# One written order for the step from the mixer's output to the feed-forward part

## The chip, the core and the metric

The kernel runs on one core of a Trainium2 chip. TensorE multiplies matrices, VectorE and ScalarE work on tiles, GpSimd does some element work and issues some of the loads, SyncE issues the others. Five engines run side by side, each through its own queue in order. The metric is the device time of one execution in microseconds; lower is better.

## The reference, cut to what matters

One layer over 256 tokens of width 2048, in float32. `attn` and `ssm` are the two halves of the mixer, `rms_norm` divides by the root of the mean square over the width and multiplies by a weight per feature.

```python
mixed = jnp.concatenate([attn, ssm], axis=-1) @ w_out[l]
x = x + rms_norm(mixed, ln_mix_post[l])
h = rms_norm(x, ln_ffn_pre[l])
u = causal_depthwise_conv(h @ w_ffn_up[l], ffn_conv_w[l], ffn_conv_b[l])
gate, up = jnp.split(u, [FFN_HIDDEN], axis=-1)
f = (jax.nn.gelu(gate, approximate=True) * up) @ w_ffn_down[l]
x = x + rms_norm(f, ln_ffn_post[l])
```

The change lies between the first line and the fourth: a product with `w_out`, a norm, a sum, a second norm, a product with `w_ffn_up`.

## The kernel before

Tokens are two tiles of 128 (`t` = 0, 1). Every product in float32 is made of three: weights and features are each split into a high and a low part of a shorter format, and high x high, high x low and low x high are summed in PSUM. Weights come in units of 128 x 1024 (0.5 MB), in the order in which they are used. `Weights.split` (L60) does one unit: SyncE loads it into a raw buffer (ring of four, `raw`), ScalarE rounds it to the high part (`whi`, L63), VectorE subtracts to get the low part (`wlo`, L64); `whi` and `wlo` are rings of four too. `tick()` follows each unit that TensorE has used: it fetches the next one, and issues work that was put off by a count of units (`defer`).

Two forms of product occur. `rows_part` (L253) multiplies a unit with token tile `t`, six matmuls of 512 columns, the output being tokens x 512 features; a chunk of 512 output features takes eight units of `w_out`. `cols_part` (L180) gives 128 output features x 256 tokens: for each of 16 slices of the width a matmul of 512 columns (high and low features of both token tiles) and one of 256. `cols_tok` (L187) does the same by token tile: one matmul of 256 columns for tile 0, two for tile 1. An up tile (`cols_tile`) takes two units.

The output `mixed` is made in four chunks. While they run, `post` (L738) squares and sums each (ScalarE) and multiplies it by the norm's weight into `mm` (VectorE). GpSimd multiplies `mm` by the second norm's row `lnrow` for three chunks of token tile 1 (`weighted`, L772). In the last chunk `rows_staggered` (L275) holds eight units: first all of token tile 0, then token tile 1. To hold eight, the chunk's first four units go to buffers of their own (`own`, L732). `last_post` (L744) is what follows for one token tile: the last sum of squares, the factor 1/rms (`late_rsqrt`: VectorE, a power on GpSimd, VectorE), `x1 = mm * r + x` in four pieces, and times `lnrow`: for token tile 0 on GpSimd (L761), for token tile 1 from the parts made ahead on GpSimd (L752, L768). `features` (L779) transposes a piece in four on TensorE (L782), ScalarE copies the high part out and VectorE the low part (L171, L172). The factor of the second norm is the same for a whole token and so is applied after the up product: `second_rms` (L785) finds it, `along_tokens` (L156) spreads it along the tokens (`rb2`) with two transposes on TensorE. `cols_pair` (L235) begins the first two up tiles with token tile 0; `gated` (L866) does convolution and gelu of a pair.

What sets the order: the code is written as one sequence, and a planner puts each engine's instructions into its queue, by the written order among those that it reckons to be ready; it may therefore run later work first. `tc.issue_after(i)` keeps instructions behind `i` on its engine. At the kernel's end the last chunk of the feed-forward output uses `rows_staggered` too, and `fdone` writes each token tile out.

## Time and profile before

| what | value |
|---|---|
| time, median of 3 runs | 1140.27 us (1140.26 to 1141.01) |
| the profiled execution | 1140.66 us |
| its span, first to last instruction | 1138.90 us |
| TensorE busy in the span | 99% |
| VectorE busy | 792.9 us, 70% |
| ScalarE busy | 592.9 us, 52% |
| GpSimd busy | 30.8 us, 3% |
| mean granted TensorE clock | 0.997 of full speed |

The span is that of one profiled execution; 1.76 us of that execution lie outside it. Busy shares are means over stages: what a stage waits for is read from the waits and the sequence in it. The last output chunk runs from about 359 to 383 us of the span, the first up tiles from 387 us on. TensorE's weight loads run beside its matmuls and have rows of their own (PEld). Matmuls overlap in the pipeline, so the time from one start to the next is the price of one, not the duration shown.

### The profile page before, as it was taken

The numbers are of one execution on the slowest core, as the hardware profiler recorded it, in microseconds if no ns is written. First come the engines' busy times: TensorE is split into PE (matmuls) and PEld (weight loads), VectorE is DVE, ScalarE is ACT, GpSimd is POOL, SyncE is SP. The second block draws the span as 40 slices with busy tenths as digits, with TensorE's granted clock in tenths as the row PEclk, the third lists the DMA queues.
The fourth block names the chain that finished last, engine by engine and source line by source line (L and its number), as shares of the span: only waits on it lengthen the run. The fifth ranks groups of instructions, "written<-read, shape, count | busy, mean of one in ns | idle before, by whom it ended". The sixth has DMA issues, their size and how long they took to land.

```text
span 1138.9 us, 15739 instructions
## 1 busy us (share of the span) xinstructions
PE 1127.2 (99%) x5896; PEld 957.2 (84%) x5896; DVE 792.9 (70%) x1250; ACT 592.9 (52%) x913; POOL 30.8 (3%) x32
## 2 busy tenths in 40 slices
PE   9999999999999899999999999999999999999997
PEld 7877888888888788888888888888888888888886
DVE  6587886776655988777878644447878787865562
ACT  6555544554454575555555444335555555554451
POOL 0000000000010500000000000000000000000000
PEclk9999999999999999999999999999999999999999
DMA  8756444555597275566656556656556656656662
GB/s 306 281 167 199 140 155 137 184 168 167 171 329 238 75 245 186 185 187 187 190 190 189 185 186 188 189 194 186 185 187 186 191 188 191 186 185 186 189 216 74
DMA packets 60148, 215.53 MB, mean 189 GB/s; under 512 B 7119, under 2 KB 7800, under 8 KB 59176
## 3 DMA queue, kind: packets, MB, share of 16 engines
q1 hardware_dynamic: 58696, 207.69, 57.2%
q0 software_dynamic: 1088, 6.48, 1.6%
q8 instruction: 46, 0.75, 0.3%
q10 hardware_dynamic: 288, 0.35, 0.1%
q14 instruction: 30, 0.25, 0.1%
HBM read 212.39 MB, written 2.11 MB: 188 GB/s over the span
## 4 chain that ended last, share of the span: by engine, by line
PE 94%; DVE 2%; DMA 2%; issue 1%; ACT 1%; SPq 0%; POOL 0%; POOLq 0%; ACTq 0%; DVEq 0%
PE pa L183 36%; PE pa L184 18%; PE pa L258 8%; PE pa L260 8%; PE pa L259 8%; PE ph L259 4%; PE ph L260 4%; PE ph L258 4%; DVE wlo L64 1%; DMA raw<-in_wout_dram 1%; PE pab L183 1%; PE pa L191 1%; DMA raw<-in_win_dram 1%; PE py L567 1%; PE pab L184 1%
## 5 line engine op out<-in xcount | busy, mean ns | idle before, releaser
L64 DVE TENSOR_TENSOR wlo<-raw,whi 128x1024 fp32r<-128x1024 f32 (+1 forms) x377 | 465.2, 1235 | 261.1 <-ACT whi L63 260.4
L63 ACT CAST whi<-raw 128x1024 fp32r<-128x1024 f32 (+1 forms) x377 | 395.1, 1048 | 455.6 <-PE pa L183 174.6
L183 PE MATMUL pa<-h,whi 128*128 128x512 f32 x1376 | 483.3, 394 | 0.0
L184 PE MATMUL pa<-h,wlo 128*128 128x256 f32 x1376 | 389.2, 283 | 0.0
L183 PEld LDWEIGHTS pa<-h,whi 128*128 128x128 f32 x1376 | 258.4, 188 | 59.6
L184 PEld LDWEIGHTS pa<-h,wlo 128*128 128x128 f32 x1376 | 258.7, 188 | 0.0
L183 PE MATMUL pa<-hT,whi 128*128 128x512 f32 x384 | 138.5, 399 | 0.0
L184 PE MATMUL pa<-hT,wlo 128*128 128x256 f32 x384 | 108.2, 283 | 0.0
L823 DVE SCALAR_TENSOR_TENSOR cfc<-cfu,fcv,cfc 128x255 f32<-128x255 f32 (+1 forms) x176 | 84.7, 481 | 4.5 <-ACT cfc L821 1.5
L183 PEld LDWEIGHTS pa<-hT,whi 128*128 128x128 f32 x384 | 72.2, 188 | 16.6 <-issue 0.2
L184 PEld LDWEIGHTS pa<-hT,wlo 128*128 128x128 f32 x384 | 72.1, 188 | 0.3 <-issue 0.2
L260 PE MATMUL pa<-whi,gT 128*128 128x512 f32 x176 | 69.5, 395 | 0.0
L258 PE MATMUL pa<-whi,gT 128*128 128x512 f32 x176 | 69.4, 395 | 0.0
L259 PE MATMUL pa<-wlo,gT 128*128 128x512 f32 x176 | 69.4, 394 | 0.0
L259 PE MATMUL ph<-wlo,gT 128*128 128x512 f32 x160 | 63.1, 395 | 0.0
L260 PE MATMUL ph<-whi,gT 128*128 128x512 f32 x160 | 63.1, 395 | 0.0
L258 PE MATMUL ph<-whi,gT 128*128 128x512 f32 x160 | 63.1, 395 | 0.0
L821 ACT ACTIVATE cfc<-cfu,fcv 128x256 f32<-128x256 f32 x88 | 52.6, 597 | 1.4 <-DVE cfu L820 1.4
L258 PE MATMUL pa<-whi,hT 128*128 128x512 f32 x128 | 51.7, 404 | 0.2 <-DVE xsT L200 0.2
L260 PE MATMUL pa<-whi,hT 128*128 128x512 f32 x128 | 50.7, 396 | 0.0
L259 PE MATMUL pa<-wlo,hT 128*128 128x512 f32 x128 | 50.6, 395 | 0.0
L258 PE MATMUL pa<-whi,mT 128*128 128x512 f32 x112 | 43.9, 392 | 0.0
(242 smaller groups left out, 1183.6 us busy)
## 6 DMA issues: line engine op xcount, KB each, us to landing
raw<-in_wup_dram SPq DMA_DIRECT2D x176, 512.0 KB, 3.5
raw<-in_wdown_dram SPq DMA_DIRECT2D x88, 512.0 KB, 3.5
raw<-in_win_dram SPq DMA_DIRECT2D x87, 512.0 KB, 3.5
raw<-in_wout_dram SPq DMA_DIRECT2D x32, 512.0 KB, 4.3
xsq<-in_x_dram SPq DMA_DIRECT2D x2, 1024.0 KB, 7.8
xt<-in_x_dram POOLq DMA_DIRECT2D x2, 1024.0 KB, 7.5
xr<-in_xT_dram SPq DMA_DIRECT2D x7, 256.0 KB, 6.2
out_dram<-xt SPq DMA_DIRECT2D x6, 256.0 KB, 2.4
```

The source lines that it names most:

```text
L63: nc.scalar.copy(hi[:, s], raw[:, s])
L64: nc.vector.tensor_tensor(lo[:, s], raw[:, s], f32(hi[:, s]), op=ALU.subtract)
L183: nc.tensor.matmul(ps, w[0][:, s], aT[:, k, :, :], start=(k == 0), stop=False)
L184: end[0] = nc.tensor.matmul(ps[:, :S], w[1][:, s], aT[:, k, 0, :], start=False, stop=(k == KT - 1)).ins
L191: nc.tensor.matmul(both, w[0][:, s], aT[:, k, :, tok(t)], start=(t == 0 and k == 0), stop=False)
L258: nc.tensor.matmul(ps, a, w[0][:, s], start=(first and j == 0), stop=False)
L259: nc.tensor.matmul(ps, a, w[1][:, s], start=False, stop=False)
L260: end[0] = nc.tensor.matmul(ps, b, w[0][:, s], start=False, stop=(last and j == 1)).ins
L567: nc.tensor.matmul(py[:, i * 64:(i + 1) * 64], rows[:, t, g, i, :], xcs[t, g][:, i * 64:(i + 1) * 64], start=True, stop=True)
L821: nc.scalar.activation(c, u, AF.Identity, scale=wv[:, 2:3], bias=wv[:, 3:4])
L823: nc.vector.scalar_tensor_tensor(c[:, sh:], u[:, :S - sh], wv[:, 2 - sh:3 - sh], c[:, sh:], op0=ALU.mult, op1=ALU.add)
```

## The change

The step from the last output chunk to the third up tile is written out as one sequence for TensorE, ScalarE and VectorE inside `tc.manual_schedule`, which fixes their order. All products with `lnrow` go to VectorE: those of x are made in place (`x_weighted`), put off by two to nine units; those of `mm` right behind it (`weighted`, into `ml`). Then `scaled` gives a piece of features with one instruction. GpSimd makes no products any more. The rings of `whi` and `wlo` get three more buffers from the last output stage on, to the kernel's end (`deepen`); the raw ring keeps four; the separate buffers go, in both places. The last chunk holds five units instead of eight (`HOLD`), at the kernel's end too. Three up tiles are begun with token tile 0 instead of two, the third in a buffer of another PSUM pool. As `x_weighted` overwrites x, x is loaded a second time behind the sequence, and `second_rms` then makes x1 and its squares. The spreading of the second norm's factor stands ahead of the up tiles in the code, without a count of units. ScalarE's scaling of the last norm's row is put off by twelve units.

```diff
+HOLD = 5
+MORE = {"raw": 0, "whi": 3, "wlo": 3}
 class Weights:
+    def deepen(self, pool):
+        self.more, self.base, self.behind = pool, self.fetched, MORE["whi"]
+    def rounded(self, raw, hi, lo, i, s):
         nc.sync.dma_start(out=raw[:, s], in_=self.units[i][:, s])
         nc.scalar.copy(hi[:, s], raw[:, s])
-        nc.vector.tensor_tensor(lo[:, s], raw[:, s], f32(hi[:, s]), op=ALU.subtract)
+        return lambda: nc.vector.tensor_tensor(lo[:, s], raw[:, s], f32(hi[:, s]),
+                                               op=ALU.subtract)
+    def place(self, i, n, bufs, dtype):
+        pool = self.pool
+        if self.more and (i - self.base) % (bufs + MORE[n]) < MORE[n]:
+            pool, bufs = self.more, MORE[n]
+        return pool.tile([P, UE], dtype, name=n, tag=n, bufs=bufs)
     def fetch(self):
-        while self.fetched < len(self.units):
...
+        if self.fetched < len(self.units):
+            self.fetch_rounded()()
+    def tick(self):
+        self.fetch()
+        if self.behind:
+            self.behind -= 1
+            self.fetch()
...
-    def cols_pair(pss, aT):
...
-    def rows_staggered(pss, aT, kts, done, late, first=True):
...
+    def rows_to_tail(pss, aT, kts, first=True):
+        n = len(kts) - HOLD
         for i in range(n):
             w = ws.take()
             for t in range(NT):
                 rows_part(pss[t], w, aT, kts[i], t, first and i == 0, False)
             tick()
+        return [ws.take() for _ in range(HOLD)]
+    def rows_tail(pss, aT, kts, tail, t, j):
+        rows_part(pss[t], tail[j], aT, kts[len(kts) - HOLD + j], t, False, j == HOLD - 1)
...
+        ws.deepen(ctx.enter_context(tc.tile_pool(name="wq", bufs=1, side="right")))
...
-        own = [px.tile([P, 4, UE], F32R, name=f"own{c}") for c in "hl"]
+        ml = px.tile([P, NT, D], F32, name="ml")
...
+        def weighted(t, c):
+            nc.vector.tensor_tensor(ml[:, t, chunk(c)], mm[:, t, chunk(c)], lnrow[:, chunk(c)],
+                                    op=ALU.mult)
+        def x_weighted(t, c):
+            nc.vector.tensor_tensor(xt[:, t, chunk(c)], xt[:, t, chunk(c)], lnrow[:, chunk(c)],
+                                    op=ALU.mult)
         def post(c):
             def fn(t, ps):
                 square_sum(ss[0][t][:, c:c + 1], ps)
                 nc.vector.tensor_tensor(mm[:, t, chunk(c)], ps, wpost[:, chunk(c)], op=ALU.mult)
+                weighted(t, c)
...
+        def factor(t, ps):
             square_sum(ss[0][t][:, 3:4], ps)
+            return late_rsqrt(ss[0][t][:, 3:4], early[t], lambda: nc.vector.tensor_tensor(
+                mm[:, t, chunk(3)], ps, wpost[:, chunk(3)], op=ALU.mult))
+        def scaled(t, q):
+            h = ml[:, t, chunk(q)]
+            nc.vector.scalar_tensor_tensor(h, h, rs[t], xt[:, t, chunk(q)], op0=ALU.mult,
+                                           op1=ALU.add)
+        def turned(t, q):
             pt = psum("pxt").rearrange("p (j c) -> p j c", c=P)
             for j in range(4):
+                nc.tensor.transpose(pt[:, j, :], ml[:, t, q * 512 + j * P:q * 512 + j * P + P],
+                                    ident)
+            dst = [h2[:, q * 4:q * 4 + 4, c, tok(t)] for c in range(2)]
+            last = [nc.scalar.copy(dst[0], pt).ins]
+            def rest():
+                last.append(nc.vector.tensor_tensor(dst[1], pt, f32(dst[0]), op=ALU.subtract).ins)
+            return rest, last
...
+        for t in range(NT):
+            for c in range(4):
+                defer(2 + t * 4 + c, x_weighted, t, c)
...
+        pss = chunk_psums()
+        tail = rows_to_tail(pss, mT, both)
+        held_up = [col_psum(), col_psum(), psum("pq")]
+        def first_tokens(q):
+            for i, ps in enumerate(held_up):
+                for k in range(q * 4, q * 4 + 4):
+                    cols_tok(ps, units[k // 8 * 3 + i], h2, k, k % 8, 0)
...
+        with tc.manual_schedule(engines={E.PE, E.Activation, E.DVE}):
+            for j in range(HOLD):
+                rows_tail(pss, mT, both, tail, 0, j)
+            rs.append(factor(0, pss[0]))
+            scaled(0, 0)
+            scaled(0, 1)
+            weighted(0, 3)
+            scaled(0, 2)
+            t1_units(0, 1)
+            more = [ws.fetch_rounded()]
+            t1_units(1, 2)
+            more.append(ws.fetch_rounded())
+            t1_units(2, 3)
+            turn(0, 0)
+            turn(0, 1)
+            finish(0, 0)
+            finish(0, 1)
+            scaled(0, 3)
+            t1_units(3, 4)
+            more.append(ws.fetch_rounded())
+            t1_units(4, 5)
+            rs.append(factor(1, pss[1]))
+            more.append(ws.fetch_rounded())
+            units.extend(ws.take() for _ in range(6))
+            turn(0, 2)
+            first_tokens(0)
+            turn(0, 3)
+            scaled(1, 0)
+            finish(0, 2)
+            first_tokens(1)
+            scaled(1, 1)
+            finish(0, 3)
+            turn(1, 0)
+            first_tokens(2)
+            turn(1, 1)
+            finish(1, 0)
+            more[0]()
+            finish(1, 1)
+            first_tokens(3)
+            scaled(1, 2)
+            weighted(1, 3)
+            more[1]()
+            second_tokens(0)
+            turn(1, 2)
+            scaled(1, 3)
+            more[2]()
+            finish(1, 2)
+            more[3]()
+            second_tokens(1)
+            turn(1, 3)
+            finish(1, 3)
+            second_tokens(2)
+            second_tokens(3)
+        for t in range(NT):
+            aux(out=xt[:, t, :], in_=x[0, tok(t), :])
+        tick()
+        came = rest[1, 3][1]
+        with tc.issue_after(came[0]), tc.issue_after(came[1]):
+            for _ in range(5):
+                tick()
+            sums = second_rms()
...
+        if half == 0:
+            along_tokens(rb2, [sums[:, t:t + 1] for t in range(NT)])
         for i in range(half * HALF, (half + 1) * HALF):
...
-            own = pers.tile([P, 4, 2, UE], F32R, name="own", tag="h", bufs=1)
+            begun = held_up[2 * i:2 * i + 2]
+            pg, pu = begun + [col_psum() for _ in range(2 - len(begun))]
+            for ps in (pg, pu)[len(begun):]:
+                cols_tile(ps, h2)
+            gated(i, pg, pu)
...
-    wup[:4] = wup[[0, 2, 1, 3]]
+    wup[:6] = wup[[0, 2, 4, 1, 3, 5]]
```

`second_tokens` is `first_tokens` with token tile 1; `t1_units(a, b)` runs `rows_tail` for token tile 1; `turn` calls `turned` and `finish` its `rest`.

## Rows read from the trace of the kernel before

**Rows 1.** The page, engines: busy us, share of the span, instructions.

```profile
PE 1127.2 (99%) x5896; PEld 957.2 (84%) x5896; DVE 792.9 (70%) x1250; ACT 592.9 (52%) x913; POOL 30.8 (3%) x32
```

**Rows 2.** TensorE's waits: what waited for whom, us in total, times, longest.

```profile
PE pxt L782 <- POOL hl L761: 2.4, 1, 2.4
...
PE pa L191 <- DVE h L172: 1.0, 1, 1.0
```

**Rows 3.** Stretches: length, busy us of PE, PEld, DVE, ACT, POOL; clock, DMA, GB/s.

```profile
359.00:370.00 11.00, 11.00 (x50) 9.12 (x49) 4.77 (x9) 3.27 (x6) 1.29 (x1) 1.00 0.66 226
...
387.00:391.00 4.00, 4.00 (x22) 4.00 (x22) 3.93 (x10) 2.17 (x6) 0.80 (x2) 0.57 0.38 136
391.00:402.00 11.00, 11.00 (x94) 10.79 (x93) 9.16 (x15) 7.11 (x15) 1.16 (x2) 1.00 0.32 111
```

**Rows 4.** Timeline, TensorE: start, us, instruction, count, idle before and its releaser.

```profile
370.02 0.39 PE L258 MATMUL pa<-whi,mT 128*128 128x512 f32 x1
...
378.19 0.60 PE L782 MATMUL pxt<-cst,hl 128*128 128x128 f32 x4
...
378.86 0.40 PE L259 MATMUL pa<-ownl,mT 128*128 128x512 f32 x1
...
382.31 0.40 PE L260 MATMUL pa<-ownh,mT 128*128 128x512 f32 x1
385.10 0.66 PE L782 MATMUL pxt<-cst,hl 128*128 128x128 f32 x4 [2.39 <-POOL hl L761]
386.78 4.76 PE L191 MATMUL pa<-h,whi 128*128 128x256 f32 x25 [1.02 <-DVE h L172]
391.38 0.60 PE L782 MATMUL pxt<-cst,hl 128*128 128x128 f32 x4
...
397.10 0.28 PE L194 MATMUL pa<-h,wlo 128*128 128x256 f32 x1
...
401.73 0.39 PE L183 MATMUL pa<-h,whi 128*128 128x512 f32 x1
...
407.34 0.38 PE L160 MATMUL prb<-cst,rsr 128*128 128x128 f32 x2
```

**Rows 5.** Timeline, VectorE, around the boundary.

```profile
357.29 2.51 DVE L64 TENSOR_TENSOR wlo<-raw,whi 128x1024 fp32r<-128x1024 f32 x2 [0.64 <-ACT whi L63]
...
361.61 0.68 DVE L741 TENSOR_TENSOR mm<-pa,wpost 128x512 f32<-128x512 f32 x1
...
372.39 4.83 DVE L756 SCALAR_TENSOR_TENSOR xt<-mm,lsr,xt 128x512 f32<-128x512 f32 x4
377.15 8.97 DVE L64 TENSOR_TENSOR wlo<-raw,whi 128x1024 fp32r<-128x1024 f32 x4
386.04 1.87 DVE L172 TENSOR_TENSOR h<-pxt,h 128x512 fp32r<-128x512 f32 x3
...
395.69 1.41 DVE L756 SCALAR_TENSOR_TENSOR xt<-mm,lsr,xt 128x512 f32<-128x512 f32 x2
```

**Rows 6.** GpSimd's products: ns min/median/max, first and last start.

```profile
L761 POOL TENSOR_TENSOR hl<-xt,lnrow x4: 1742/1992/2264, 373.2 to 382.8; 128x512 f32<-128x512 f32 x4
```

**Rows 7.** DMA issues (KB, us to landing), and ScalarE's wait for one.

```profile
lnrow<-in_vec_dram POOLq DMA_DIRECT2D x1, 1024.0 KB, 15.6
...
raw<-in_wup_dram SPq DMA_DIRECT2D x176, 512.0 KB, 3.5
...
324.47 1.92 ACT L729 ACTIVATE wpost<-wpost 128x2048 f32<-128x2048 f32 x1 [2.15 <-DMA wpost<-in_vec_dram]
```

**Rows 8.** Timeline, VectorE, last chunk's token tile 0.

```profile
1120.14 0.21 DVE L149 TENSOR_SCALAR lsa<-ss,esb 128x1 f32<-128x1 f32 x1 [8.09 <-ACT junk L166]
...
1121.51 2.74 DVE L862 SCALAR_TENSOR_TENSOR xt<-fa,lsr,xt 128x512 f32<-128x512 f32 x4
```

**Rows 9.** Timeline: a load issued on GpSimd's queue, and its user.

```profile
397.81 0.54 POOL L810 DMA_DIRECT2D wpo<-in_vec_dram  x1
...
402.96 1.92 ACT L811 ACTIVATE wpo<-wpo 128x2048 f32<-128x2048 f32 x1 [0.25 <-DMA wpo<-in_vec_dram]
```

More of the change, by code (lines that the diff above doesn't have):

```diff
@@ L57, in __init__ @@
         self.nc, self.pool, self.units = nc, pool, units
-        self.fetched, self.ready, self.place = 0, [], {}
+        self.fetched, self.ready, self.more, self.base, self.behind = 0, [], None, 0, 0
+    def deepen(self, pool):
+        self.more, self.base, self.behind = pool, self.fetched, MORE["whi"]
     def split(self, raw, hi, lo, i, s):
+        self.rounded(raw, hi, lo, i, s)()
+    def rounded(self, raw, hi, lo, i, s):
         nc = self.nc
@@ L208, in tick @@
     def tick():
-        ws.fetch()
+        ws.tick()
         for p in pending:
@@ L282, in rows_staggered @@
             tick()
-        tail = [ws.take() for _ in range(8)]
-        for t, order in ((0, range(8)), (1, (4, 5, 6, 7, 0, 1, 2, 3))):
-            for o, j in enumerate(order):
-                rows_part(pss[t], tail[j], aT, kts[n + j], t, first and n == 0 and o == 0, o == 7)
-                if t == 1:
-                    if j >= 4:
-                        tick()
-                    if o in late:
-                        late[o]()
-            done(t, pss[t])
+        return [ws.take() for _ in range(HOLD)]
+    def rows_tail(pss, aT, kts, tail, t, j):
+        rows_part(pss[t], tail[j], aT, kts[len(kts) - HOLD + j], t, False, j == HOLD - 1)
     ws = Weights(nc, wp, [win[i] for i in range(win.shape[0])]
@@ new lines, in decoder_layer, with second_tokens @@
+        tail = rows_to_tail(pss, mT, both)
+        held_up = [col_psum(), col_psum(), psum("pq")]
+        rs, rest, units = [], {}, []
+        def first_tokens(q):
+            for i, ps in enumerate(held_up):
+                for k in range(q * 4, q * 4 + 4):
+                    cols_tok(ps, units[k // 8 * 3 + i], h2, k, k % 8, 0)
+        def second_tokens(q):
+            for i, ps in enumerate(held_up):
+                for k in range(q * 4, q * 4 + 4):
+                    cols_tok(ps, units[k // 8 * 3 + i], h2, k, k % 8, 1)
@@ new lines, in t1_units, with turn, finish @@
+        def t1_units(a, b):
+            for j in range(a, b):
+                rows_tail(pss, mT, both, tail, 1, j)
+        def turn(t, q):
+            rest[t, q] = turned(t, q)
+        def finish(t, q):
+            rest[t, q][0]()
+        E = mybir.EngineType
+        with tc.manual_schedule(engines={E.PE, E.Activation, E.DVE}):
[51 more added lines that the diff above has]
+            second_tokens(3)
@@ L897, in decoder_layer @@
                 fearly += [early_sum(ss[2][t][:, :3]) for t in range(NT)]
-                rows_staggered(held[1], gT, range(0, HALF, 2), fdone(1, 3), {}, first=False)
+                kts = range(0, HALF, 2)
+                tail = rows_to_tail(held[1], gT, kts, first=False)
+                for t in range(NT):
+                    for j in range(HOLD):
+                        rows_tail(held[1], gT, kts, tail, t, j)
+                    fdone(1, 3)(t, held[1][t])
             else:
```

89 lines of the change are left out of this document (12 added, 77 removed).

## The prediction

> **What bounds the kernel now.** I read the views in this order: the engines' busy time, TensorE's list of waits, the granted clock by stretch, and then TensorE's own sequence around the boundary. TensorE is busy for 1127.2 of 1138.9 us [rows 1], so only a time in which it stands still, or runs slowly, can be won. The list of waits says where that is: the boundary has two entries of a microsecond or more, 2.4 us for a product that GpSimd makes and 1.0 us for an evacuation by VectorE [rows 2]. Right behind them the clock falls: 0.57 of full speed in 387 to 391 us, which is mostly the 1.2 GHz level, against 1.00 in 391 to 402 [rows 3].
>
> **What the boundary loses, worked out from TensorE's sequence [rows 4].**
> Unit prices first. A 512-column matmul: 36 of them lie between 370.02 and 378.19, so 0.227 each. A 256-column matmul: 39 starts from 397.10 to 401.73, so 0.119. A group of four transposes: 378.19 to the second matmul behind it at 378.86 is 0.67, less one matmul 0.44.
> - Token tile 1 of the last output chunk should take 48 x 0.227 + 3 x 0.44 = 12.22 us from 370.02; its last matmul starts at 382.31, so its turn ends at 382.54, after 12.52: 0.30 lost.
> - The next group of transposes could start at 382.54 and starts at 385.10: 2.56 lost (the GpSimd product).
> - It should be over at 385.54; the first up matmul starts at 386.78: 1.24 lost (the evacuation).
> - 25 up matmuls run from 386.78 to 391.38, 4.60 us; at 0.119 they would need 2.97: 1.63 lost to the clock.
> - From 391.38 to 401.73 there are 71 matmuls and four groups of transposes, 8.45 + 1.76 = 10.21 against 10.35: 0.14 lost.
> Sum: 5.87 us. All of it lies on the path, since TensorE has next to no slack behind it.
>
> **The change, part by part.**
> *TensorE's work* stays the same but for its order: eight groups of transposes in both kernels; three up tiles begun by token tiles instead of two. The third one costs 48 x 0.119 = 5.71 in this order, against 5.61 in the plain order (401.73 to 407.34) [rows 4]: 0.10 more.
>
> *The written order.* With five held units instead of eight, token tile 0 is complete after 3 x 2.72 + 5 x 1.36 = 15.0 us of the chunk (six matmuls of 0.227 are 1.36) instead of 10.9. I count from that moment. TensorE then has 5 x 1.36 = 6.8 us for token tile 1, 8 x 0.44 = 3.5 for transposes, 48 x 0.119 = 5.7 of first-token and 96 x 0.119 = 11.4 of second-token matmuls, together 27.5 us. The question is whether VectorE keeps ahead. Its prices where GpSimd makes no products: a scaled sum 0.70 (two in 1.41), the rest of an evacuation 0.62 (three in 1.87), the low part of a weight unit 1.25 (two in 2.51), a product 0.68 [rows 5]. The factor of a token tile is there 2.4 us after its last matmul (370.02 to 372.39) [rows 4, 5]. I laid these one behind the other in the written order, ScalarE's copies between them; here is when each value is there, against when TensorE wants it:
> - first two transposes: at 3.1 and 3.8, wanted at 4.1 and 4.5.
> - first-token matmuls: features at 6.1, 6.7, 11.4, 12.7; wanted at 8.2, 10.0, 11.9, 13.8.
> - transposes of token tile 1: 10.8, 12.1, 16.0, 18.4; wanted at 11.5, 13.3, 18.1, 21.4.
> - second-token matmuls: the low part of the third unit at 14.6, wanted at 15.2; the last low part at 21.4, wanted at 21.8; the last features at 23.4, wanted at 24.7.
> No wait, and the least margin is 0.4 us, at the last low part, because VectorE has hardly a gap from 2.3 to 21.4. What the switches to fresh tiles cost: the losses of 0.30 and 0.14 above lie at seven groups of transposes, the worse at 0.10 a group; the bounds for eight are 0 and 0.8; I take 0.3, nearer to 0, as most tiles are now made well ahead.
>
> *Products ahead on VectorE.* Eight for x, eight for the output: 16 x 0.68 = 10.9 us more on VectorE, and all but two of them lie beside the output chunks, where it is busy 4.8 of 11 us [rows 3] and TensorE's matmuls cover them. GpSimd loses its ten products (four of them 1.7 to 2.3 us each [rows 6]). One danger: the products for x wait for the row of weights, whose load lands 15.6 us after its issue as the last of four of 1 MB, and stand ahead of weight splits on VectorE; three more units, 1.5 MB, are fetched in that time. At the rate of those four, 0.26 MB a us, that puts the row off by at most 6 us. Before, ScalarE waited 2.2 us for the row ahead of it and TensorE, with four units in hand, lost nothing [rows 7]; with seven it has 7 x 2.72 = 19 us in hand. I take 0; without that cover it is up to 6.
>
> *Ring of seven, the separate buffers gone, at both ends.* The six units that the three tiles need are loaded before the block and split in it. The buffer for the next unit's raw data comes free at 14.6 with the third unit's low part, a load takes 3.5 us [rows 7], so it is there by 19, split by about 24.5, wanted at 27.5. SyncE's queue holds only such loads, in order. At the kernel's end token tile 0 is ready 6.8 us ahead of token tile 1 instead of 10.9; what follows it on VectorE takes 1120.14 to 1124.25, 4.1 us [rows 8]: still hidden, 0.
>
> *The reload of x and the second norm.* x has been overwritten, so 2 MB are loaded again on GpSimd's queue, token tile 0 after 7.4 us and token tile 1 after 18.4; behind them stand the constants of the feed-forward part and the power of the second norm. A 1 MB load on that queue was issued at 397.81 and its user ran at 402.96 [rows 9]; so x is there by about 24. Eight scaled sums and sums of squares come after 23.4, between splits: six splits are done by about 32, as their loads wait for each other's raw buffers, the sums need 8 x 0.70 = 5.6, and the last square and the factor some 2.4 as above. So the factor is there at 40 at the latest. Its two transposes cost nothing as long as they stand behind that moment in TensorE's queue. A like case was: the transposes of token tile 1 were written ahead of the up matmuls, and 25 of these ran first (386.78, then 391.38) [rows 4]; the planner filled the wait. I take 0, with bounds of 0 and 2.
>
> **Sum.** 5.87 - 0.10 - 0.30 = 5.47 us gained. The profiled execution took 1140.66, its span of 1138.90 and 1.76 around it; that gives 1135.2. The median of the runs lies 0.39 below that execution: 1134.8.
>
> **Rivals.**
> 1. *VectorE is a little too slow in the block.* Its margin is 0.4 us; with all its durations 10 or 20% longer the same layout waits 0.6 or 1.8 us at the low parts, and a wait can bring the low clock of before (1.6): 1135.4 to 1138.2. For it: hardly a gap on VectorE for 19 us. Against it: the quiet price of a scaled sum is the same far apart, 0.70 at 395.69 and four in 2.74 at 1121.51 [rows 5, 8].
> 2. *VectorE's slow durations stay.* In the boundary of before four scaled sums took 4.83, 1.21 each, and four low parts 8.97, 2.24 each [rows 5]. If that comes from the work around them and not from GpSimd, the layout waits 6.2 us (0.4, 1.4 and 4.4), with or without 1.6 for the clock: 1141.0 to 1142.6, no gain. Against it: the slow ones lie where GpSimd ran its products [rows 5, 6], and the quiet ones at 395.69 lie in the same boundary behind them. The Trainium skill bears on this, "SBUF — State Buffer", section "Who interferes with whom": a VectorE instruction with two SBUF inputs and a GpSimd instruction that reads SBUF exclude each other from a shared port. By that rule rival 2 falls, since GpSimd keeps only powers of 128 x 1; the trace agrees in direction, 0.70 against 1.21.
> 3. *Slower: the second norm's transposes stand in TensorE's queue ahead of the next up tile.* They would wait from 27.5 to 40, 12.5 us, and 1.6 for the clock: 1148.9. It decides from a wait of 3.9 us on (1140.3 - 1134.8 - 1.6). For it: before, a count of two units held them back, now nothing does, and x has to be loaded first. Against it: the planner's order at 386.78. The same page of the Trainium skill (section "SBUF: two separate sides") warns that loads issued on GpSimd starve beside some VectorE work, which would add to this wait; the load of rows 9 was used after 5.2 us in a stretch where VectorE was busy 9.2 of 11 us [rows 3].
> 4. *The change doesn't do what it says: the next units come late.* If the eight scaled sums go ahead of the next unit's low part on VectorE, that is there at 23.3 + 5.6 + 1.25 = 30.2 instead of 24.5, TensorE waits 2.7 us from 27.5 and the clock takes 1.6: 1139.1. For it: the order there is the planner's. Against it: the first of these splits is written ahead of the sums.
>
> **How the numbers follow.** Forecast 0.64, rival 1 0.14, rival 2 0.07, rival 3 0.10, rival 4 0.05. The range 1134.2 to 1139.2 takes in the forecast with its bounds and rivals 1 and 4 (0.83). A measurement of this kernel can tell 0.2%, 2.3 us, from no change. Faster, below 1138.0: 0.64 + 0.14 = 0.78. Within: rivals 2 and 4, 0.12. Slower: rival 3, 0.10.
>
> **What would show it.** Right: TensorE's list of waits has nothing above 0.5 us at the boundary; the granted clock stays at 1.00 through it; VectorE's scaled sums there take 0.75 and the low parts 1.2; the second-token matmuls follow each other without a gap. Wrong: a TensorE wait for a low part or for features (rival 1 or 2, told apart by VectorE's durations), a wait of the transposes for the second norm's factor (3), or of the first plain up tile for a low part (4).

## The result, and the profile after

The changed kernel takes 1148.37 us (median of 4 runs, 1148.18 to 1149.41), the kernel before 1140.42 (4 runs, 1140.26 to 1141.01): ratio 1.0071, 95% interval 1.0053 to 1.0088. It is slower by 8 us, clear of the interval, where 5.5 us of gain were forecast. The profiled execution took 1148.41 us, its span is 1146.6. The experiments ran on other chips, so below a variant is always given by its ratio to the kernel before on its own chip.

The page's engines after, to be read against [rows 1]: VectorE has 3.5 us more to do, GpSimd 17.7 less.

```profile
PE 1129.6 (99%) x5912; PEld 958.4 (84%) x5912; DVE 796.4 (69%) x1270; ACT 591.4 (52%) x913; POOL 13.1 (1%) x24
```

TensorE's waits in the changed kernel (who waited for whom, us in total, times, longest). Both entries of [rows 2] are gone; two new ones stand in their place. `cfu` at L219 is an add that empties the PSUM buffer of a finished up tile; `prb` are the two transposes that spread the second norm's factor, `rsr` is that factor.

```profile
PE pa L202 <- DVE cfu L219: 5.3, 2, 3.5
PE prb L179 <- DVE rsr L148: 3.2, 1, 3.2
```

TensorE's timeline of the changed kernel (start, us, instruction, idle before and its releaser): two units of weights in the chunk before the last, the start of the last chunk, the first matmul behind the three up tiles, the two longer waits, and the first matmul behind the last output matmul.

```profile
346.13 0.39 PE L265 MATMUL pa<-whi,mT 128*128 128x512 f32 x1
...
348.93 0.39 PE L265 MATMUL pa<-whi,mT 128*128 128x512 f32 x1
...
359.99 0.39 PE L265 MATMUL pa<-whi,mT 128*128 128x512 f32 x1
...
402.35 0.39 PE L202 MATMUL pa<-h,whi 128*128 128x512 f32 x1
...
413.49 0.28 PE L203 MATMUL pa<-h,wlo 128*128 128x256 f32 x1
417.28 0.47 PE L202 MATMUL pa<-h,whi 128*128 128x512 f32 x1 [3.51 <-DVE cfu L219]
...
423.59 0.43 PE L179 MATMUL prb<-cst,rsr 128*128 128x128 f32 x2 [3.16 <-DVE rsr L148]
...
1137.96 1.25 PE L933 MATMUL pa<-xt,cst 128*128 128x256 f32 x6
```

The same two ends in the kernel before, the start of the last chunk and the first matmul behind the last output matmul:

```profile
359.14 0.39 PE L258 MATMUL pa<-ownh,mT 128*128 128x512 f32 x1
...
1130.22 1.25 PE L851 MATMUL pa<-xt,cst 128*128 128x256 f32 x6
```

Two differences give the balance. The three up tiles are done at 402.35, before at 407.34 [rows 4]: 4.99 us won up to there. From there to the end of TensorE's output matmuls took 722.9 us before (407.34 to 1130.22) and takes 735.6 now (402.35 to 1137.96): 12.7 us lost behind it. 12.7 - 5.0 = 7.7, the whole result. Of the 12.7, 5.3 + 3.2 = 8.5 are the waits above. The other 4.2 are about what the low clock behind these waits costs: some 14 pairs of one 512- and one 256-column matmul take 0.64 us each there instead of 0.35 (418.31 to 418.95, against 402.35 to 402.71), an estimate of 4.1.

The 4.99 is itself a balance. The last chunk starts at 359.99 instead of 359.14, so 0.85 us is lost ahead of it; from its start to the end of the third up tile TensorE takes 42.36 us instead of 48.20, so the sequence itself won 5.84. Some 0.5 of the 0.85 comes from the three new buffers: in the output stage three units of weights in seven take 2.80 us (346.13 to 348.93) where all took 2.72 before. These are the units that lie in the new buffers; why their matmuls are slower no run shows.

The changed kernel by stretches (columns as in [rows 3]; before the last two numbers, DMA share and GB/s, stands the granted clock):

```profile
374.00:382.00 8.00, 8.00 (x40) 6.64 (x39) 5.36 (x11) 4.82 (x7) 0.56 (x1) 1.00 0.01 3
382.00:389.00 7.00, 7.00 (x58) 6.77 (x57) 5.44 (x11) 3.28 (x6) 1.14 (x2) 1.00 0.40 152
...
395.00:410.00 15.00, 15.00 (x109) 14.04 (x109) 8.37 (x9) 5.44 (x8) 1.06 (x2) 1.00 0.95 356
...
415.00:420.00 5.00, 2.72 (x9) 2.33 (x10) 5.00 (x7) 4.97 (x11) 0.00 (x0) 0.77 0.43 125
420.00:425.00 5.00, 1.84 (x10) 1.23 (x9) 4.03 (x10) 2.65 (x6) 0.72 (x1) 0.84 0.98 357
425.00:430.00 5.00, 5.00 (x23) 4.37 (x22) 2.73 (x6) 2.46 (x4) 0.00 (x0) 0.70 0.73 221
...
435.00:440.00 5.00, 3.16 (x14) 2.79 (x14) 5.00 (x12) 2.51 (x6) 0.00 (x0) 0.82 0.47 116
```

From the start of the written order up to 410 us TensorE works without a gap at 1.00 (2.4 GHz): the forecast gain is there. From 415 on the clock is 0.77, 0.84 and 0.70, mixtures with the 1.2 GHz level; TensorE had stood still for 3.5 us just before, and stands again for 3.2. The third wait, 1.8 us for the second add, ends at 436.87, and behind it the clock falls once more (0.82).

Why the factor is late is on VectorE. Its timeline in the changed kernel: `ml` at L764 is the first scaled sum of the written order, `wlo` the low part of a weight unit (the one at 388.48 is the first of four that the written order postpones), L784 is x1 (eight pieces, which the second norm squares and sums), L788 its last sum, L148 the factor, L219 an add that frees PSUM.

```profile
377.52 1.42 DVE L764 SCALAR_TENSOR_TENSOR ml<-ml,lsr,xt 128x512 f32<-128x512 f32 x2
...
388.48 1.22 DVE L73 TENSOR_TENSOR wlo<-raw,whi 128x1024 fp32r<-128x1024 f32 x1
...
398.38 0.74 DVE L784 SCALAR_TENSOR_TENSOR xt<-mm,lsr,xt 128x512 f32<-128x512 f32 x1
399.04 1.22 DVE L73 TENSOR_TENSOR wlo<-raw,whi 128x1024 fp32r<-128x1024 f32 x1
403.58 1.23 DVE L73 TENSOR_TENSOR wlo<-raw,whi 128x1024 fp32r<-128x1024 f32 x1 [3.32 <-ACT whi L72]
406.78 1.23 DVE L73 TENSOR_TENSOR wlo<-raw,whi 128x1024 fp32r<-128x1024 f32 x1 [1.97 <-ACT whi L72]
407.92 0.75 DVE L784 SCALAR_TENSOR_TENSOR xt<-mm,lsr,xt 128x512 f32<-128x512 f32 x1
...
414.07 2.73 DVE L784 SCALAR_TENSOR_TENSOR xt<-mm,lsr,xt 128x512 f32<-128x512 f32 x4
416.72 0.42 DVE L219 TENSOR_TENSOR cfu<-pa,cfu 128x256 f32<-128x256 f32 x1
417.05 4.62 DVE L73 TENSOR_TENSOR wlo<-raw,whi 128x1024 fp32r<-128x1024 f32 x4
421.59 0.15 DVE L788 TENSOR_REDUCE sum<-ss 128x2 f32<-128x8 f32 x1
...
423.38 0.16 DVE L148 TENSOR_TENSOR rsr<-rsy,rsq 128x2 f32<-128x2 f32 x1
```

The first piece of x1 runs at 398.38, the second 9.5 us later: between them stand low parts whose high parts ScalarE has not made, and VectorE works its queue in order. The add that TensorE waits for until 417.28 stands behind the eighth piece, at 416.72. ScalarE in the same stretch (timeline; L72 rounds a unit to its high part, L185 squares, L235 scales the post-norm row):

```profile
402.50 1.05 ACT L72 CAST whi<-raw 128x1024 fp32r<-128x1024 f32 x1 [4.04 <-DMA raw<-in_wup_dram]
...
409.08 1.05 ACT L72 CAST whi<-raw 128x1024 fp32r<-128x1024 f32 x1 [2.06 <-DMA raw<-in_wup_dram]
410.04 1.92 ACT L235 ACTIVATE wpo<-wpo 128x2048 f32<-128x2048 f32 x1
...
420.54 0.63 ACT L185 ACTIVATE junk<-xt 128x512 f32<-128x512 f32 x1
```

So ScalarE waits for raw data, VectorE for ScalarE, and then both catch up: the last square starts at 420.54, 3.7 us behind the last piece of x1 (414.07 + 2.73). The loads themselves are slow from 395 to 410 us, when the DMA engines are busy to 0.95. The DMA issues of that stretch (KB, median us to landing):

```profile
raw<-in_wup_dram SPq DMA_DIRECT2D x6, 512.0 KB, 9.5
wpo<-in_vec_dram POOLq DMA_DIRECT2D x1, 1024.0 KB, 10.6
```

A weight unit took 3.5 us in the kernel before, and the 1 MB row 5.2 us from its issue to its user [rows 7, 9]. From 374 to 382 us, on the other hand, almost nothing was loaded (share 0.01). That fits a raw ring without a free buffer: it has four, and the low parts of the four units that the written order postpones run only from 388.48 us on.

### The profile page after: what moved, and what is told of

Same layout as the page of the kernel before. It is cut to its first block, busy times and chain, and to the rows that moved or that the text cites. A ratio compares the mean times of both kernels' runs of the same rounds, so it can differ in the third digit from the quotient of the medians.

```text
span 1146.6 us, 15787 instructions
## 1 busy us (share of the span) xinstructions
PE 1129.6 (99%) x5912; PEld 958.4 (84%) x5912; DVE 796.4 (69%) x1270; ACT 591.4 (52%) x913; POOL 13.1 (1%) x24
## 4 chain that ended last, share of the span: by engine, by line
PE 94%; DMA 2%; DVE 2%; ACT 1%; issue 1%; POOL 0%; SPq 0%; POOLq 0%; ACTq 0%
PE pa L202 34%; PE pa L203 18%; PE pa L265 9%; PE pa L266 9%; PE pa L267 9%; PE ph L267 4%; PE ph L265 4%; PE ph L266 4%; DMA raw<-in_wup_dram 2%; PE pab L202 1%; DVE wlo L73 1%; PE pab L203 1%; PE py L568 1%; DMA raw<-in_win_dram 0%; ACT whi L72 0%
## 5 line engine op out<-in xcount | busy, mean ns | idle before, releaser
L72 ACT CAST whi<-raw 128x1024 fp32r<-128x1024 f32 (+1 forms) x385 | 402.9, 1047 | 475.4 <-PE pa L202 222.8
L203 PE MATMUL pa<-h,wlo 128*128 128x256 f32 x1360 | 385.1, 283 | 0.0
L267 PE MATMUL ph<-whi,gT 128*128 128x512 f32 x176 | 69.3, 394 | 0.0
L265 PE MATMUL ph<-whi,gT 128*128 128x512 f32 x176 | 69.2, 393 | 0.0
L266 PE MATMUL ph<-wlo,gT 128*128 128x512 f32 x176 | 69.2, 393 | 0.0
L265 PE MATMUL pa<-whi,mT 128*128 128x512 f32 x128 | 50.5, 394 | 0.0
```

Of the source, the lines that this page charges most:

```text
L72: nc.scalar.copy(hi[:, s], raw[:, s])
L203: end[0] = nc.tensor.matmul(ps[:, :S], w[1][:, s], aT[:, k, 0, :], start=False, stop=(k == KT - 1)).ins
L265: nc.tensor.matmul(ps, a, w[0][:, s], start=(first and j == 0), stop=False)
L266: nc.tensor.matmul(ps, a, w[1][:, s], start=False, stop=False)
L267: end[0] = nc.tensor.matmul(ps, b, w[0][:, s], start=False, stop=(last and j == 1)).ins
```

## Experiments

In each of the first four one thing that may be late is taken away: the second load of x, the place of the adds behind the second norm, the load of the post-norm row, and then the last two together with a later place for what needs the factor. Two theories were put up: L, that the loads are what costs, and Q, that the order on VectorE is.

**e1, no second load of x.**

```diff
-        for t in range(NT):
-            aux(out=xt[:, t, :], in_=x[0, tok(t), :])
```

> The changed kernel without its second load of x (2 MB); what goes into the last residual sum is then x times the row of weights, so this part of the computation is left out. Theory L (loads): in 395 to 410 us the memory system is full, weight units land late, ScalarE's roundings wait for them in its queue (8.2 us) and the second norm stands behind. L expects these waits under 4 us, the second norm's factor at least 4 us earlier than 423.5, TensorE's three waits (8.5 us) down to 3 or less, and 1136 to 1141. Theory Q (order): the two additions that free the first pair's PSUM buffers stand behind the second norm on VectorE whatever the loads do. Q expects both waits for them, 5.3 us, nearly unchanged, and 1144 to 1148.

Measured: ratio 1.0039 (1.0025 to 1.0053). ScalarE's waits for raw data fell from 8.2 to 3.7 us and the factor came at 419.99 instead of 423.38, but TensorE still waits 4.8 us for it at the transposes, and 1.8 for an add. The time is in Q's range, but the waits for adds did not stay as Q expected. The loads are part of the lateness, not all of it.

**e2, the adds of the first pair written ahead of the second norm.**

```diff
+    for f, ps in zip((0, NF), held_up):
+        summed[f] = fp.tile([P, S], F32, name="cfu", tag="cf", bufs=8)
+        cols_sum(summed[f], ps)
     tick()
     came = rest[1, 3][1]
     with tc.issue_after(came[0]), tc.issue_after(came[1]):
```

> The changed kernel, with the two additions that free the first pair's PSUM buffers written ahead of the next units' splits and of the second norm; all loads as they were. Q expects both waits for them gone, 5.3 us and most of the low clock behind them, the wait of the two transposes for the factor still there: 1139 to 1143. L expects that TensorE only reaches the transposes sooner and waits there instead, 6 us or more in that one wait: 1144 to 1148.

Measured: 1.0036 (1.0023 to 1.0049). The adds run at 408.60 and 410.80 instead of 416.72 and 427.83 and TensorE's wait for them shrinks from 5.3 to 0.6 us; the wait at the transposes grows from 3.2 to 7.7. The factor comes at 423.46, as it did. One wait took over from the other, as L expected.

**e3, the post-norm row loaded late**, behind the ninth product of the feed-forward part.

```diff
-    aux(out=wpo, in_=row_bcast(V_FFNPOST, D))
-    defer(12, nc.scalar.mul, wpo, wpo, -0.5)
...
+        if i == 8:
+            nc.vector.tensor_copy(wpo[:, :1], cu[:, :1])
+            aux(out=wpo, in_=row_bcast(V_FFNPOST, D))
+            defer(12, nc.scalar.mul, wpo, wpo, -0.5)
```

> The changed kernel, with the load of the last norm's row (1 MB, beside the second load of x) made to wait until pair 8 is through; it is needed only in the second half. L expects about half of what leaving out the load of x gives: 1142 to 1146. Q expects no more than 1 us: 1147 to 1149.

Measured: 1.0038 (1.0024 to 1.0052). Waits for raw data 5.6 us, factor at 420.77, and again 5.2 us at the transposes and 2.6 for adds. The time is in L's range.

**e4, e2 and e3 together, and what needs the factor put off by six weight units**: the transposes, and the convolutions of the first two pairs, whose adds stay where the tile ends. Work put off by a count of units is also kept behind the last matmul of the unit it counts to (`tc.issue_after` in `tick`), so the planner can't run it earlier.

```diff
-            along_tokens(rb2, [sums[:, t:t + 1] for t in range(NT)])
+            defer(6, along_tokens, rb2, [sums[:, t:t + 1] for t in range(NT)])
...
-            gated(i, pg, pu)
+            if i < 2:
+                for f, ps in ((i, pg), (NF + i, pu)):
+                    if f not in summed:
+                        summed[f] = fp.tile([P, S], F32, name="cfu", tag="cf", bufs=8)
+                        cols_sum(summed[f], ps)
+                defer(6 - 2 * i, gated, i, pg, pu)
```

> The changed kernel with the additions first, the last norm's row late, and the two transposes of the second norm's factor put off by six units, with the convolutions of the first two pairs behind them. If order and loads together are the cause, TensorE's waits behind the written sequence are under 2 us and the time is 1135 to 1138, which is what the sequence itself won. If something else in that stretch is late (VectorE has too much to do there), waits of 3 us or more stay and it is 1139 to 1144.

Measured: 0.9993 (0.9984 to 1.0002), level with the kernel before. One wait is left, 3.2 us, and it is at the transposes; the factor came at 421.58.

In each of the four TensorE stands at the same two transposes, whatever was late before them. Taking the wait from the start of the transposes, TensorE reaches them at 415.4 (e1), 416.0 (e2), 415.8 (e3) and 418.6 (e4), 3 to 8 us ahead of the factor. Their place in its queue can be counted: behind the third up tile 37 pairs of matmuls come first in the kernel after, in e1 and in e3, 38 in e2, and 48 in e4 by its count of six units. So neither L nor Q is enough; the next theory, P, is that their place costs, and that what makes the factor late matters only because of it. Against it stands M: the loss moves on, whatever is put off.

**e6, the place of what needs the factor**: the kernel after, with the transposes put off by eight units and the convolutions of the first three pairs with them; the adds stay where each tile ends. Loads and written order stay.

```diff
-            along_tokens(rb2, [sums[:, t:t + 1] for t in range(NT)])
+            defer(8, along_tokens, rb2, [sums[:, t:t + 1] for t in range(NT)])
...
+                defer(8 - (0, 2, 6, 10)[i], gated, i, pg, pu)
```

> The kernel after, with nothing changed but the place of the factor's transposes and of the convolutions of the first three pairs: put off by eight units. Loads as they were, the adds still behind the second norm on VectorE. Theory P: the wait of 3.2 us at the transposes and its 1.4 us of low clock are gone, the waits for the adds (3.5 and 1.8) stay: 1148.4 - 4.6 = 1143.8 (1142.5 to 1145.5). Theory M: the wait is taken over in full by the adds, 1146.5 to 1149. If the adds alone were the fault, then nothing is gained here; if the place alone, 1136 to 1139.

Measured: 0.9976 (0.9966 to 0.9986), against 1.0071 without it: 0.0095 x 1140 = 10.8 us from this edit (8 to 14 by the ends of both intervals). TensorE's waits from 395 to 450 us, and the transposes (ns min/median/max, first and last start):

```profile
PE pa L202 <- DVE cfu L219: 2.4, 1, 2.4
```

```profile
L179 PE MATMUL prb<-cst,rsr x2: 272/272/273, 427.5 to 427.7; 128*128 128x128 f32 x2
```

The factor was no earlier, at 425.67; it had only stopped mattering. More went than the 4.6 us that were expected, since the wait for the second add and the slow clock around it went as well: that add stood behind the first use of the factor on VectorE (424.63 and 427.83 in the kernel after), and this edit parts the two. Some 2 us of the 10.8 are not explained by the place: the first wait for an add is 2.4 us instead of 3.5, and the clock stayed at 1.00 behind it, where it had cost 1.2. No run moves the two transposes without the convolutions, so their shares are not separated. Of 12.7 us the wait of 2.4 is left.

**e5, e4 with eight units and three pairs.** The edit of e6 on top of e2 and e3.

> The kernel after, with the adds of the first pair's tiles written ahead of the second norm, the load of the post-norm row put behind the ninth product of the feed-forward part, and the transposes of the second norm's factor (with the convolutions of the first three pairs, which need it) put off by eight weight units. Theory P (the transposes' place in TensorE's queue is what costs): in the run with six units they stood at 419.2 and waited 3.15 us, the factor came at 421.58; eight units put them about 5.7 us later, at 424.9, so no wait of TensorE and no stretch at the low clock between 405 and 445 us, and the run takes 1140.4 - 3.2 - 1.6 = 1135.6 (1134.5 to 1137.5). Theory M (the loss moves on, whatever is put off: TensorE runs out of free PSUM buffers or of split weights instead): a wait of 2 to 4 us at another place, 1139 to 1142.

Measured: 1134.91 us, ratio 0.9947 (0.9933 to 0.9960), faster than both kernels. The factor came at 423.07 and the transposes ran at 424.7 without a wait. By stretches:

```profile
415.00:420.00 5.00, 5.00 (x30) 4.38 (x29) 4.79 (x7) 4.77 (x12) 0.00 (x0) 1.00 0.59 167
420.00:425.00 5.00, 5.00 (x31) 4.40 (x30) 4.42 (x10) 3.17 (x5) 0.72 (x1) 1.00 0.88 282
```

TensorE is busy for all of 405 to 445 us at 1.00. ScalarE still waits 8.0 us for raw data (395 to 450 us), but TensorE waits for no weights. Theory P holds, and M falls for eight units.

**e8, e5 without the late row.** Only the edit of e3 is taken back.

> As the run with eight units, but with the load of the post-norm row where the kernel after has it, ahead of the feed-forward part. Theory P: the crowded loads only set when the factor is there; in the kernel after it came at 423.38 with this load, so with the transposes at about 424.9 nothing waits: 1135.6 (1134.5 to 1138). Theory L (the loads are what costs): ScalarE's casts wait for raw data as before (8 us against 7), split weights come late, and TensorE waits 2 us or more for one: 1138.5 to 1141.

Measured: 0.9960 (0.9946 to 0.9974). The factor came at 425.50 instead of 423.07 and the transposes waited 1.0 us, where P had expected no wait; the wait of 2 us for split weights that L had expected is not there. The crowded loads move the factor by 2.4 us; the intervals of e5 and e8 overlap, so what that is worth in time is not settled.

**e9, e5 with ten units.**

> As the run with eight units, with ten. Theory P: if eight are enough, ten give the same within 0.1%, since the convolutions put off further only hold values in SBUF; if the factor comes later than 424.9 in that run, ten give back what is left of the wait. Theory M: the convolutions that are put off pile up on VectorE and the adds of later pairs stand behind them: 1 to 4 us slower than with eight.

Measured: 0.9971 (0.9962 to 0.9980), 2.7 us more than with eight. The transposes at 429.9 wait for nothing, but TensorE waits 2.2 us for an add and from 440 to 445 us is busy for 2.77 of 5: here M holds, the convolutions put off stand ahead of a later add on VectorE. Of six, eight and ten units eight is the best.

**e10, the second norm ahead of the five weight units.** Why is the factor late?

```diff
-            for _ in range(5):
-                tick()
             sums = second_rms()
+            for _ in range(5):
+                tick()
```

> The kernel after, with one thing changed: the second norm's sums are written ahead of the five weight units instead of behind them. Theory S (the factor is late because its sums stand behind the low parts of weight units whose raw data come late; in the kernel after the first sum ran at 398.38 and the second only at 407.92, behind two such low parts): the sums run as soon as x is there, the factor comes at 410 to 416 instead of 423.38, the transposes wait for nothing, and what is left is a wait for the adds or for a low part of the next units: 1142 to 1146. Theory X (the second load of x sets it): the factor stays at 420 or later, and the time at 1147 to 1149.

Measured: 1.0030 (1.0019 to 1.0041). VectorE's and ScalarE's timelines in this run:

```profile
397.88 2.73 DVE L784 SCALAR_TENSOR_TENSOR xt<-mm,lsr,xt 128x512 f32<-128x512 f32 x4
402.18 2.74 DVE L784 SCALAR_TENSOR_TENSOR xt<-mm,lsr,xt 128x512 f32<-128x512 f32 x4 [1.57 <-DMA xt<-in_x_dram]
...
416.00 0.16 DVE L148 TENSOR_TENSOR rsr<-rsy,rsq 128x2 f32<-128x2 f32 x1
```

```profile
409.41 1.90 ACT L235 ACTIVATE wpo<-wpo 128x2048 f32<-128x2048 f32 x1
...
413.45 0.63 ACT L185 ACTIVATE junk<-xt 128x512 f32<-128x512 f32 x1
```

Theory S holds for the sums: all of x is there at 402.18 and x1 is finished at 404.92 instead of 416.80. The factor follows at the very end of the range expected, 416.00, because the squares on ScalarE now are late: the last one starts 8.5 us behind x1, after casts that waited for raw data and the scaling of the row. And the transposes wait 5.6 us all the same, where none was expected: the planner had moved them up as well, from behind 37 pairs of matmuls to behind 21, and TensorE reaches them at 410.7. It also waits 1.0 us for a low part, which now stands behind the sums. That the place goes with the planner's reckoning of the factor, and that this is early in both runs, fits the two places; the reckoning itself is in no trace.

**e11, GpSimd's products again.** Ten products on GpSimd on a tile of no use, added to e5 at the written order's start.

```diff
             scaled(0, 0)
+            nc.gpsimd.tensor_tensor(idle, ml[:, 0, :256], lnrow[:, :256], op=ALU.mult)
+            for _ in range(9):
+                nc.gpsimd.tensor_tensor(idle, idle, lnrow[:, :256], op=ALU.mult)
             scaled(0, 1)
```

> The run with eight units, with ten products of 128x256 added on GpSimd, on a tile that nobody uses, started with the first scaled sum of token tile 0 (about 373 us); they should fill some 10 us there. Theory G (VectorE's slow durations at the boundary of the kernel before came from GpSimd's products): the instructions of VectorE with two operands in SBUF that run beside them take 1.2 us (scaled sums) and 2.2 us (low parts) again, against 0.74 and 1.22; the written order has 0.4 us of margin, so TensorE waits 2 to 5 us in the block and 1.6 for the clock: 1138 to 1142. Theory W (they came from the rest of the work around them): durations as without the products, 1134.9 within 0.2%.

Measured: 1.0001 (0.9992 to 1.0011), 6 us more than e5. VectorE's timeline, and under it GpSimd's:

```profile
377.95 1.42 DVE L765 SCALAR_TENSOR_TENSOR ml<-ml,lsr,xt 128x512 f32<-128x512 f32 x2
379.28 1.23 DVE L742 TENSOR_TENSOR ml<-mm,lnrow 128x512 f32<-128x512 f32 x1
380.43 1.22 DVE L765 SCALAR_TENSOR_TENSOR ml<-ml,lsr,xt 128x512 f32<-128x512 f32 x1
381.58 1.27 DVE L778 TENSOR_TENSOR h<-pxt,h 128x512 fp32r<-128x512 f32 x2
...
389.46 0.22 DVE L171 SCALAR_TENSOR_TENSOR lsq<-lsy,lsa 128x1 f32<-128x1 f32 x1 [4.30 <-POOL lsy L169]
```

```profile
378.79 1.18 POOL L832 TENSOR_TENSOR idle<-ml,lnrow 128x256 f32<-128x256 f32 x1 [1.37 <-DVE ml L765]
380.04 8.24 POOL L834 TENSOR_TENSOR idle<-idle,lnrow 128x256 f32<-128x256 f32 x9
```

Theory G holds for the durations: beside GpSimd's products a product takes 1.23 us and a scaled sum 1.22, against 0.68 and 0.74 without them in e5; the next scaled sum, at 382.77, takes 0.85. The two evacuations that take one operand from PSUM (`h<-pxt,h`) stay at 1.27 together, 1.29 in e5. The Trainium skill, "SBUF — State Buffer", section "Who interferes with whom", draws the line there: a VectorE instruction with two inputs in SBUF contends with a GpSimd instruction that reads SBUF, one with at most one such input, outside the two-port modes, does not. These rows agree in direction. The time, however, was lost elsewhere: the factor of token tile 1 needs a power on GpSimd, which stood behind the ten products, so VectorE waited 4.3 us for it and TensorE 3.6 for the next features. No low part ran beside the products, so its 2.2 us of before [rows 5] were not made again.

**e12 and e13, one low part moved up**, in the kernel after and in e5.

```diff
             finish(0, 1)
             scaled(0, 3)
+            more[0]()
...
             finish(1, 0)
-            more[0]()
```

> The kernel after, with one instruction of the written order moved up on VectorE: the low part of the first of the four next units, from 388.48 us to behind the fourth scaled sum of token tile 0 (about 382.5), where VectorE waits 1.4 us anyway. Theory R (the four raw buffers are held by these postponed low parts, so nothing is loaded from 374 to 382 us, and what was not loaded then crowds with x's second load and the norm's row from 395 to 410): the next raw load starts 6 us earlier, ScalarE's casts wait 1 to 5 us for raw data instead of 8.2, the factor comes 1 to 4 us before 423.38, and the run takes 1144.5 to 1147.5. Theory B (the transfers of this stretch take their time in whatever order): casts wait 8 us as before, factor at 423 or later, 1147.5 to 1149.

> The run with eight units, with the same low part moved up. TensorE has no wait left at the boundary there, so by theory P an earlier factor gives nothing more: 1134.9 within 0.2%. Slower by 1 us or more, if the moved low part delays the factor of token tile 1, whose transposes have little margin in the written order.

Measured: e12 1.0071 (1.0057 to 1.0085), the same as without the edit; e13 0.9953 (0.9939 to 0.9966), the same as e5 within the intervals. In e12 a wait of 3.8 us, which the list puts to a high part, stands where the kernel after waits 3.5 for the first add. One stretch of e12, and a wait of TensorE that is new there and in e13:

```profile
389.00:395.00 6.00, 4.83 (x42) 4.62 (x42) 4.65 (x7) 2.20 (x4) 0.00 (x1) 1.00 0.00 0
```

```profile
PE pa L210 <- DVE h L777: 1.2, 1, 1.2
```

A unit more is loaded from 382 to 389, and then nothing from 389 to 395: the three other raw buffers are still held. Counted over the same stretch, 395 to 450 us, ScalarE's casts wait 8.6 us for raw data, 8.2 without the edit; the factor comes at 424.56. So theory R failed, and what theory B expected came in. That the held buffers are why nothing is loaded fits these rows, but freeing one does not show it; a deeper raw ring would, and no run has one.

The new wait is not the moved low part's 1.2 us of work. ScalarE's and VectorE's timelines in e12:

```profile
388.79 1.05 ACT L72 CAST whi<-raw 128x1024 fp32r<-128x1024 f32 x1 [3.36 <-DMA raw<-in_wup_dram]
389.74 1.06 ACT L774 CAST h<-pxt 128x512 fp32r<-128x512 f32 x2
...
390.35 1.29 DVE L777 TENSOR_TENSOR h<-pxt,h 128x512 fp32r<-128x512 f32 x2 [2.98 <-ACT h L774]
```

VectorE stands idle for 2.98 us there. The low part frees a raw buffer, the next unit's load starts earlier, and its cast, which is written behind the block, now stands in ScalarE's queue ahead of two evacuation copies and waits 3.36 us for its data. In the kernel after these copies ran at 387.25 and 389.11, and that cast at 393.34.

## Why the prediction was wrong

*What bounds, and the loss at the boundary* (5.87 us): right. Both waits are gone, the granted clock is 1.00 throughout, and from the start of the last chunk to the end of the third up tile 5.84 us were won, against 5.47 forecast. e5, where TensorE waits for nothing behind it, is 6.0 us faster than the kernel before (0.0053 x 1141.5), and e8, with the row's load in its old place, 4.6.

*The written order without a wait*: right. Token tile 0 is complete at about 375.15 (the first scaled sum at 377.52, less the 2.37 it took before), so the third up tile is done 27.2 us later; 27.5 was laid out. Whether the least margin is 0.4 us no run tests: the wait in e12 comes from a cast that was not in the layout.

*Products ahead on VectorE, no cost*: right; the products for x ran from 330.9 to 345.5, the row landed after 14.6 us and TensorE waited for neither. *Ring of seven*: it had no term for slower matmuls out of the new buffers, and 0.85 us were lost ahead of the last chunk, some 0.5 of it to them. *The kernel's end, no cost*: right; from the last output matmul to the end of the span it takes 8.6 us, 8.7 before.

*The reload of x and the second norm, 0 with bounds of 0 and 2*: wrong. This step, with the adds below that hang on the same chain, carries the miss: 12.7 us behind the third up tile instead of 0 to 2. Counted from 375.15:
- x is there by about 24, it said. In e10, where VectorE waits for it, the second half came at 402.18, and token tile 0 was complete at 374.73 by the same reckoning: 27.4. That is 3.4 us late, but not what set the end.
- x1 was to be finished at 32 + 5.6 = 37.6. It was finished at 41.6 (416.80): 4.0 late. I had let the loads of the units wait for each other's buffers, at the 3.5 us of a quiet stretch; they took 9.5 in a crowded one.
- The last square and the factor were to take 2.4. They took 6.7 (416.80 to 423.54): 4.3 late. The 2.4 was the price with an empty ScalarE; here its queue held casts of late units and the scaling of the row.
- So the factor stands at 48.4 instead of "at 40 at the latest". The word "latest" had no bound behind it: every price in it was that of a quiet row.
- The transposes cost nothing, it said, "as long as they stand behind that moment". The planner did put matmuls ahead of them, as the prediction expected, but not enough: 37 pairs behind the third up tile, at 0.352 a pair (402.35 to 413.25 are 31 of them) 13.0 us, so they stood at 415.4, or 40.2. That is about my own moment for the factor; it came at 48.4.
- One case in which the planner had filled a wait (the transposes of token tile 1) was taken as evidence for another. It had no loads in it. In the runs where the planner was free to place the transposes (the kernel after, e1, e2, e3, e10, e12) they stood 3 to 8 us ahead of the factor.

*What had no term at all*: the adds that free PSUM. On VectorE they were queued behind the second norm's eight pieces, and for the second tile behind the first use of the factor. They cost 5.3 us of waits; with a count of units on the users of the factor it is 2.4 (e6), and nothing when they are also written first (e5).

*The rivals.* Rivals 1 and 2 did not happen: the scaled sums took 0.71 to 0.75 us and the low parts 1.22; e11 shows that GpSimd's products do slow the first. Rival 4's mechanism, low parts late behind the sums, did not stop TensorE in the kernel after (0.2 us for a low part in the whole list of waits); in e10, where the sums go first, it cost 1.0. Rival 3 is nearest to what happened, and at its time (1148.9 forecast, 1148.4 measured), but not as told: it had the transposes directly behind the third up tile, one wait of 12.5 us and 1.6 for the clock; they stood 37 pairs of matmuls later, there were three waits with 8.5 us in sum, 5.3 of them for adds that the rival does not have, and about 4.2 for the clock. The nearness of the two numbers is luck. The rival's chance of 0.10 was far too low. The point against it was the planner alone; the points for it, that a count of two units had been taken away and that x had to come first, were facts of the change. Whether loads issued on GpSimd starve beside VectorE's work, which the prediction named there, these runs don't separate from the crowding: SyncE's loads came as late.

*What is open*: how much of the factor's lateness each load causes (e1 3.4 us, e3 2.6, e8 against e5 2.4, not additive), and whether a deeper raw ring would remove the crowding.

## What to carry to other kernels

Whenever an instruction on the bounding engine waits for a long chain, ask for its place in that engine's queue and for the latest time of the chain, priced with crowded loads and full queues; an estimate made of quiet prices was a lower bound here. Moving what needs the factor a few microseconds back was worth 10.8 us, while speeding up the chain alone (e1, e3, e10) was worth 3.6 to 4.7 and left a wait of 4.8 to 5.6 us at the same transposes. And what frees buffers (here an add of 0.42 us) belongs into the sum as much as what computes.

## What the runs showed of the hardware that was not expected

- Loads of 0.5 MB that landed after 3.5 us in the median of the kernel before took 9.5 us while the 16 DMA engines were busy to 0.95 at 356 GB/s; loads on SyncE's queue and on GpSimd's suffered alike (9.5 instead of 3.5 us, and 10.6 instead of 5.0 for the 1 MB row).
- TensorE's clock did not answer to each wait. After 3.5 us of standing still it fell to the 1.2 GHz level within half a microsecond of resuming (matmuls of 512 columns 0.59 us long instead of 0.40); after the 2.4 us in e6 and the 2.2 us in e9 it stayed at 1.00; after the 1.8 us before 436.87 in the kernel after it fell too, 1.5 us after resuming (0.63 us from 438.42 on).
- Of GpSimd's ten small products of 128x256 nine took 0.92 us each. The 6 us that they cost came less from VectorE's slower instructions than from GpSimd's queue, where they stood ahead of a power of 128x1: the one wait of TensorE in the boundary goes back to it.
- A unit of weights in one of the three new buffers took 2.80 us instead of 2.72 in the mixer's output stage, in the kernel after as in e5, e6 and e9; in the down product of the kernel after it was the other way round, 2.75 in the new buffers and 2.79 in the old. Why is open.
